# Expert-choice experts of a one-core layer: second half of an expert's inputs made inside its up projection, all down weights split

## The chip, the cores and the metric

One core of a Trainium2 chip runs one launch of the whole layer in fp32. The metric is the device time of that launch in microseconds (us). TensorE is called PE, VectorE DVE, ScalarE ACT, GpSimd POOL, and SP is the engine that issues most DMA loads.

## What is computed

One hybrid layer: a short gated convolution over 1024 tokens of width 2048, followed by 16 experts that each choose 128 tokens. Only the experts matter here.

```python
aff = softmax(h @ w_router)
g, idx = top_k(aff.T, 128)                       # 128 tokens for each of the 16 experts
xe = h[idx]                                      # (16, 128, 2048), h = modulate(rmsnorm(x))
y = (silu(xe @ w1) * (xe @ w3)) @ w2 * g         # w1, w3: 2048x1024, w2: 1024x2048 for each expert
out = rmsnorm(x + g2 * zeros.at[idx].add(y))
```

## The kernel before, in words

The weights of an expert are 48 chunks of 128 x 1024 fp32 numbers (512 KB each): 32 for the up projection, in 16 blocks of two (one of w1, one of w3), and 16 for the down projection, in two halves of 8 blocks of one. The order of all 768 chunks is up(0), up(1), down(0), up(2), down(1), ..., up(15), down(14), down(15), written out by hand; every engine runs its instructions in the order in which the program gives them.

SP loads a chunk into a buffer of a ring of 28 (`c_load`, L1142), 22 chunks ahead of its use from the third expert on, 24 to 26 ahead before. A chunk is then **split** (`c_split`, `split`): ACT rounds it to a high part (`hi`, L76), DVE subtracts that from the raw chunk for a low part (`lo`, L77). `next_chunk` keeps the splits 3 chunks ahead of the matmuls (`SL`). `use_chunk` makes six matmuls of 128 x 512 of a split chunk (L1390: two with the high part, two with the low part, two with the high part and the low part of the inputs). A few chunks are left **unsplit**: their two products go straight from the raw chunk (L1385; the profile shows each fp32 product as two matmul records). Unsplit are 16 chunks of up(0), 4 of up(1), the two of block 1 in every later up projection, and block 7 of each half of every down projection (`NATD = 7`), 32 chunks in all of the down projections.

The inputs of an expert are picked by `select` (DVE compares slot numbers with positions, `oh`, L1318; PE turns that into token numbers, L1321), fetched by `gather` (two indirect DMAs of POOL, L1336, 1024 columns each), scaled by `gathered` (ACT, L1342) and turned by `xe_part`. One `xe_part` makes a quarter, 512 of the 2048 input columns: four PE transposes (L1359), four ACT activations that modulate (`xe`, L1376), one ACT cast (`hi<-xe`, L76) and one DVE subtraction (`lo<-xe`, L77). The first two quarters serve blocks 0 to 7 of the up projection, the last two blocks 8 to 15. Quarters 0 and 2 also take three buffers from the ring of 28.

Such steps hang as hooks behind a block. In down(e), behind blocks 3 and 5, the rows of expert e+2 are scaled; behind blocks 7, 9, 11 and 13 its four quarters are made. In up(e), behind block 8, `select(e+1)` runs, behind block 12 `gather(e+1)`, behind blocks 13 and 14 `hid_part(e-1)`, which turns the middle activations of the expert before (L1409 to L1416). `gate_up` (L1398, L1399) ends an up projection; behind each half of a down projection DVE weights the result (`y`, L1462) and POOL adds it to the stream in DRAM (L1468). In the start, up(0) scales the rows of expert 1 behind its last block, and the four quarters of expert 1 stand between up(0) and up(1). The last rows of the stream are read back (L1561), combined and normalised behind the last expert.

Of the kernel before, what the change touches and what calls it, by code (L numbers as in the profile page):

```python
# [7 lines left out]
F32 = mybir.dt.float32  # L8
# [7 lines left out]
P = 128  # L16
N = 1024
D = 2048
E = 16
F = 1024  # L20
# [3 lines left out]
KF = F // P  # L24
# [10 lines left out]
def hybrid_layer(ctx: ExitStack, tc: tile.TileContext, x, c, w_ada, b_ada, norm_g, w_in, w_conv, w_out,  # L35
                 w_router, w1, w3, w2, final_g, out):
    nc = tc.nc
# [9 lines left out]
    def slot(dtype=F32, name="s", tag="s"):  # L47
        return slots.tile([P, 1024], dtype, name=name, tag=tag, bufs=TAGS[tag])
# [12 lines left out]
    def acc_bank():  # L61
        return psum.tile([P, 512], F32, name="acc", tag="acc", bufs=6)

    def tr_bank():
        return psum.tile([P, 512], F32, name="tr", tag="tr", bufs=2)
# [7 lines left out]
    def split(raw, hi=None, lo=None):  # L73
        hi = part("hi") if hi is None else hi
        lo = part("lo") if lo is None else lo
        nc.scalar.copy(hi, raw)  # L76
        nc.vector.tensor_sub(lo, raw, hi.bitcast(F32))  # L77
        return hi, lo
# [491 lines left out]
    def emit(jp, i):  # L570
        t, b = conv[1].pop(i), conv[2].pop(i)
        nc.vector.tensor_mul(t, b, t)
        nc.gpsimd.dma_start(zd[2 * jp + i], t)
# [93 lines left out]
    for s in range(8):  # L667
        def f(s=s):
            if s:
                make_lo(0, ORDER[s - 1])  # L670
            if s < 7:
                make_sum(0, ORDER[s])
                make_hi(0, ORDER[s])
# [221 lines left out]
    mp = ctx.enter_context(tc.tile_pool(name="moe", bufs=2))  # L895
# [4 lines left out]
    ps = tr_bank()  # L900
# [205 lines left out]
    chunks = []  # L1106
# [6 lines left out]
    def down_chunks(e):  # L1113
        for hf in range(2):
            for k in range(KF):
                chunks.append((w2, e * F * D + k * P * D + hf * 1024, D, k == NATD))


    NAT = (1,)
    NAT1 = (1, 5)  # L1120
    NATD = 7
    NAT0 = (1, 3, 5, 7, 9, 11, 13, 15)
    up_chunks(0)
    for e in range(1, E):
        up_chunks(e)
        down_chunks(e - 1)
    down_chunks(E - 1)

    def is_nat(i):
        return chunks[i][3]  # L1130
# [5 lines left out]
    def c_load(tag="s"):  # L1136
        i = nload[0]
        if i >= len(chunks):
            return
        src, off, stride, _ = chunks[i]  # L1140
        t = slot(name="craw", tag=tag)
        nc.sync.dma_start(t, dram(src, off, [stride, P], [1, 1024]))  # L1142
        craw[i] = t
        nload[0] += 1

    def c_split():
        i = nsplit[0]
        if i >= len(chunks):
            return
        if not is_nat(i):  # L1150
            chl[i] = split(craw.pop(i))
        nsplit[0] += 1
# [176 lines left out]
    def half_rows(name):  # L1329
        return own(name)  # L1330

    def gather(e):
        idx = info[e][1]
        xg[e] = [half_rows("xg") for _ in range(2)]
        for hf in range(2):
            nc.gpsimd.indirect_dma_start(out=xg[e][hf], out_offset=None, in_=x1d[hf][:, :],  # L1336
                                         in_offset=bass.IndirectOffsetOnAxis(ap=idx[:, :1], axis=0))

    def gathered(e, hf, b=None):
        g = xg[e][hf] if b is None else xg[e][hf][:, b * 512:(b + 1) * 512]  # L1340
        if e:
            nc.scalar.activation(g, g, AF.Copy, scale=info[e][0][:, 3:4])  # L1342
        else:
            nc.vector.tensor_scalar(g, g, info[e][0][:, 3:4], None, op0=OP.mult)
# [4 lines left out]
    def xe_part(e, b, quick=False):  # L1349
        if b == 0:  # L1350
            xe[e] = []
        if b % 2 == 0:
            xe[e].append([slot(name="xe"), slot(F32R, "hi"), slot(F32R, "lo")])
        t, hi, lo = xe[e][b // 2]
        g = xg[e][b // 2]
        ps = tr_bank()
        for i in range(4):
            k = (4 * b + i) % 8
            nc.tensor.transpose(ps[:, i * P:(i + 1) * P], g[:, k * P:(k + 1) * P], ident)  # L1359
        if quick:  # L1360
            for i in range(5):
                if i < 4:
                    k = 4 * b + i
                    s = slice((k % 8) * P, (k % 8 + 1) * P)
                    nc.vector.tensor_scalar(t[:, s], ps[:, i * P:(i + 1) * P], G2[:, k:k + 1], S2[:, k:k + 1],
                                            op0=OP.mult, op1=OP.add)
                    nc.scalar.copy(hi[:, s], t[:, s])  # L1367
                if i:
                    k = 4 * b + i - 1
                    s = slice((k % 8) * P, (k % 8 + 1) * P)  # L1370
                    nc.vector.tensor_sub(lo[:, s], t[:, s], hi[:, s].bitcast(F32))
            return
        for i in range(4):
            k = 4 * b + i
            s = slice((k % 8) * P, (k % 8 + 1) * P)
            nc.scalar.activation(t[:, s], ps[:, i * P:(i + 1) * P], AF.Identity, bias=S2[:, k:k + 1],  # L1376
                                 scale=G2[:, k:k + 1])
        s = slice((b % 2) * 512, (b % 2 + 1) * 512)
        split(t[:, s], hi[:, s], lo[:, s])

    def use_chunk(i, banks, sf, sh, sl, first, last):
        if is_nat(i):
            w = craw.pop(i)
            for b in range(2):
                mm(banks[b], sf, w[:, b * 512:(b + 1) * 512], start=first, stop=last)  # L1385
            return
        wh, wl = chl.pop(i)
        for w, a, f, l in ((wh, sh, first, False), (wl, sh, False, False), (wh, sl, False, last)):
            for b in range(2):
                mm(banks[b], a, w[:, b * 512:(b + 1) * 512], start=f, stop=l)  # L1390

    hmid, hT2, hnat = {}, {}, {}

    def gate_up(e, ab, ub):
        hm = slot(name="hm", tag="w")
# [6 lines left out]
    def hid_part(e, b):  # L1402
        if b == 0:
            hT2[e] = (slot(F32R, "hh"), slot(F32R, "hl"))
        hh, hl = hT2[e]
        hm = hmid[e]
        ps = tr_bank()
        for i in range(4):
            nc.tensor.transpose(ps[:, i * P:(i + 1) * P], hm[:, (4 * b + i) * P:(4 * b + i + 1) * P], ident)  # L1409
        n = 384 if NATD // 4 == b else 512  # L1410
        s = slice(b * 512, b * 512 + n)
        nc.scalar.copy(hh[:, s], ps[:, :n])
        nc.vector.tensor_sub(hl[:, s], ps[:, :n], hh[:, s].bitcast(F32))
        if n < 512:
            hnat[e] = mp.tile([P, P], F32, name="hn")
            nc.scalar.copy(hnat[e], ps[:, n:])  # L1416

    step = [0]

    def kcap(i):  # L1420
        return 26 if i < 32 else 24 if i < 64 else K

    def next_chunk():
        i = step[0]
        step[0] += 1
        while nsplit[0] <= min(i + SL, len(chunks) - 1):
            c_split()
        for _ in range(2):
            if nload[0] - i < kcap(i):
                c_load()  # L1430
        return i
# [14 lines left out]
    def seg_down(e, hooks, emit):  # L1446
        hh, hl = hT2[e]
        for hf in range(2):
            yb = [acc_bank() for _ in range(2)]
            for k in range(KF):  # L1450
                s = slice(k * P, (k + 1) * P)
                use_chunk(next_chunk(), yb, hnat[e], hh[:, s], hl[:, s], k == 0, k == KF - 1)
                for f in hooks.get(8 * hf + k, ()):
                    f()
            emit(hf, yb)
        hT2.pop(e)
# [42 lines left out]
    def up_hooks(e):  # L1499
        h = {k: [] for k in range(KD)}  # L1500
        if e < E:
            h[8].append(lambda: select(e))
            h[KG].append(lambda: gather(e))
        h[KH].append(lambda: hid_part(e - 2, 0))
        h[KH + 1].append(lambda: hid_part(e - 2, 1))
        return h

    h = {k: [] for k in range(KD)}
# [5 lines left out]
    h[9].append(place_1)  # L1514
    h[10].append(place_2)
    h[11] += [lambda: select(1), lambda: gather(1)]
    h[15] += [lambda: gathered(1, 0), lambda: gathered(1, 1)]
    seg_up(0, h)
    for b in range(4):
        xe_part(1, b)  # L1520
    h = up_hooks(2)
    g2b = [slot(name="g2b", tag="a") for _ in range(2)]
    for b in range(4):
# [2 lines left out]
    for e in range(E - 2):  # L1526
        h = {k: [] for k in range(16)}
        h[3].append(lambda: gathered(e + 2, 0))
        h[5].append(lambda: gathered(e + 2, 1))
        for b in range(4):  # L1530
            h[7 + 2 * b].append(lambda b=b: xe_part(e + 2, b))
        down_scatter(e, h)
        seg_up(e + 2, up_hooks(e + 3))

# [2 lines left out]
    oht = slot(F32R, "oht")  # L1537
    h = {k: [] for k in range(16)}
    h[3].append(lambda: hid_part(L, 0))
    h[4].append(lambda: hid_part(L, 1))  # L1540

# [90 lines left out]
    h = {k: [] for k in range(16)}  # L1632
# [3 lines left out]
    h[13].append(lambda: combine_0(0))  # L1636
    h[15].append(lambda: combine_0(1))
    seg_down(L, h, last_emit)

    for ch in range(NC_ + 2):  # L1640
# [32 lines left out]
```

## Time and profile before

| | |
|---|---|
| time, median of 3 runs | 2727.5 us (2726.78 to 2733.08) |
| the profiled execution's own time | 2732.52 us |
| its span, first to last instruction | 2730.4 us |
| mean granted TensorE clock | 0.983 |
| busy share of PE, DVE, ACT, POOL | 97%, 76%, 54%, 11% |
| up(0) ends, up(1) starts in it | 1559.67, 1567.36 us |

A row of the chain or of a timeline has the start in us from the span's start, the duration in us, the engine with the line of the kernel, and the count of merged instructions; in brackets the idle time before it and what ended it. A PE record's duration is modelled and overlaps the next; distances between starts are exact.

### The profile page before, as it was taken

How to read it: one execution, taken by the hardware profiler on the slowest of the kernel's cores; microseconds unless marked ns; L12 is line 12 of the kernel's file. 1: busy time of each engine (PE TensorE's matmuls, PEld its weight loads, DVE VectorE, ACT ScalarE, POOL GpSimd, SP SyncE). 2: the span in 40 equal slices, each digit the busy share in tenths (PEclk: the TensorE clock that was granted, in tenths of full speed). 3: DMA queues.
4: the chain of work that ended last, by engine and by line, in shares of the span. 5: the costliest groups of instructions: out<-in, count | busy, mean ns of one | idle time of the engine just before them, and what ended most of it. 6: DMA issues, size and time to landing. Idle time of an engine off the chain costs nothing. (4 is left out here: it accounts for less than half of the span.)

```text
span 2730.4 us, 34249 instructions
## 1 busy us (share of the span) xinstructions
PE 2638.1 (97%) x11641; PEld 2067.4 (76%) x11641; DVE 2078.0 (76%) x2635; ACT 1484.3 (54%) x2142; POOL 291.4 (11%) x319
## 2 busy tenths in 40 slices
PE   6899999989999999999999899999999999999997
PEld 3588778767887887888887577777777777777775
DVE  4688788747877776676567678888888888888887
ACT  6533344423333333333343577777777777777775
POOL 1000111101111010100011000111111101111001
PEclk8899999999999999999998999999999999999999
DMA  9477777686777657897677689999999999999996
GB/s 357 153 240 240 253 271 264 241 318 187 203 203 192 179 121 228 292 301 267 217 266 247 242 324 383 374 373 375 375 372 376 373 372 374 374 373 382 375 347 246
DMA packets 321791, 795.25 MB, mean 291 GB/s; under 512 B 28256, under 2 KB 116224, under 8 KB 321616
## 3 DMA queue, kind: packets, MB, share of 16 engines
q1 hardware_dynamic: 283600, 665.54, 66.1%
q0 software_dynamic: 35728, 127.33, 17.0%
q8 instruction: 91, 1.49, 0.2%
q14 instruction: 84, 0.69, 0.1%
q10 hardware_dynamic: 2288, 0.21, 0.1%
HBM read 699.64 MB, written 93.33 MB: 290 GB/s over the span
## 5 line engine op out<-in xcount | busy, mean ns | idle before, releaser
L77 DVE TENSOR_TENSOR lo<-craw,hi 128x1024 fp32r<-128x1024 f32 x688 | 815.9, 1222 | 90.2 <-ACT hi L76 61.0
L532 PE MATMUL acc<-sh,wp 128*128 128x512 f32 x2872 | 777.6, 396 | 21.4 <-DVE c L617 7.1
L76 ACT CAST hi<-craw 128x1024 fp32r<-128x1024 f32 x688 | 694.9, 1051 | 181.1 <-PE acc L1390 177.0
L532 PEld LDWEIGHTS acc<-sh,wp 128*128 128x128 f32 x2872 | 544.4, 190 | 152.2 <-DVE c L617 11.1
L518 DVE TENSOR_TENSOR wp<-win,wp 128x512 fp32r<-128x512 f32 x336 | 231.5, 689 | 163.0 <-ACT wp L514 160.3
L514 ACT CAST wp<-win 128x512 fp32r<-128x512 f32 x336 | 207.4, 621 | 256.0 <-PE acc L532 122.9
L1390 PE MATMUL acc<-hi 128*128 128x512 f32 x928 | 306.1, 411 | 0.9 <-ACT hi L1367 0.9
L1390 PE MATMUL acc<-lo,hi 128*128 128x512 f32 x928 | 289.5, 393 | 3.4 <-DVE lo L77 1.7
L1390 PE MATMUL acc<-hi,lo 128*128 128x512 f32 x928 | 286.8, 390 | 0.0
L190 DVE SCALAR_TENSOR_TENSOR ada_acc<-wa,silu_c,ada_acc 128x512 f32<-128x512 f32 x338 | 252.9, 749 | 38.7 <-DMA wa<-w_ada 27.7
L612 ACT COPY c<-acc 128x512 f32<-128x512 f32 x156 | 91.6, 587 | 250.1 <-PE acc L532 250.1
L532 PE MATMUL acc<-sl,wp 128*128 128x512 f32 x572 | 224.6, 393 | 0.0
L1390 PEld LDWEIGHTS acc<-lo,hi 128*128 128x128 f32 x928 | 173.1, 188 | 47.1 <-DVE lo L77 11.0
L1390 PEld LDWEIGHTS acc<-hi 128*128 128x128 f32 x928 | 171.2, 189 | 47.8 <-issue 16.7
L925 PE MATMUL acc<-hi 128*128 128x512 f32 x512 | 204.0, 399 | 0.0
L1390 PEld LDWEIGHTS acc<-hi,lo 128*128 128x128 f32 x928 | 174.5, 188 | 37.9
L926 PE MATMUL acc<-lo,hi 128*128 128x512 f32 x512 | 199.6, 390 | 1.4 <-DVE lo L77 1.4
L927 PE MATMUL acc<-hi,lo 128*128 128x512 f32 x512 | 199.7, 390 | 0.0
L77 DVE TENSOR_TENSOR lo<-woraw,hi 128x1024 fp32r<-128x1024 f32 x96 | 116.9, 1220 | 98.6 <-ACT hi L76 50.4
L1390 PE MATMUL acc<-lo,hh 128*128 128x512 f32 x448 | 142.2, 399 | 5.5 <-DVE lo L77 5.5
L1390 PE MATMUL acc<-hi,hh 128*128 128x512 f32 x448 | 144.9, 404 | 0.0
L532 PE MATMUL acc<-sa,wp 128*128 128x512 f32 x576 | 140.8, 393 | 0.0
(246 smaller groups left out, 3206.5 us busy)
## 6 DMA issues: line engine op xcount, KB each, us to landing
craw<-w SPq DMA_DIRECT2D x768, 512.0 KB, 10.2
wa<-w_ada SPq DMA_DIRECT2D x128, 512.0 KB, 6.8
win<-conv_w_in SPq DMA_DIRECT2D x96, 512.0 KB, 6.5
woraw<-conv_w_out SPq DMA_DIRECT2D x96, 512.0 KB, 6.0
wa<-w_ada SPq DMA_DIRECT2D x128, 256.0 KB, 6.0
psums<-c POOLq DMA_DIRECT2D x48, 512.0 KB, 4.4
c<-psums POOLq DMA_DIRECT2D x32, 512.0 KB, 7.7
sh<-sd SPq DMA_DIRECT2D x24, 512.0 KB, 10.8
```

The costliest lines, as they stand in the source:

```text
L76: nc.scalar.copy(hi, raw)
L77: nc.vector.tensor_sub(lo, raw, hi.bitcast(F32))
L190: nc.vector.scalar_tensor_tensor(acc, t[:, a], silu_c[:, k:k + 1], acc, op0=OP.mult, op1=OP.add)
L514: nc.scalar.copy(v3(t[:, :512]), source(u, p))
L518: nc.vector.tensor_sub(v3(lo), source(u, p), v3(hi).bitcast(F32))
L532: mm(bank, w[:, c], a, start=start and q == qs[0] and i == 0, stop=q == qs[-1] and i == 2, skip_group_check=True)
L612: nc.scalar.copy(dst, bk)
L925: mm(bank, zh[:, zs], wh[:, ws], start=k == 0, stop=False)
L926: mm(bank, zh[:, zs], wl[:, ws], start=False, stop=False)
L927: mm(bank, zl[:, zs], wh[:, ws], start=False, stop=k == KD - 1)
L1390: mm(banks[b], a, w[:, b * 512:(b + 1) * 512], start=f, stop=l)
```

## The change

No chunk of a down projection is left unsplit, so block 7 of each half is split like the others. `hid_part` therefore makes the high and low part of all 512 columns and loses the extra copy (L1416). Quarters 0 and 1 of an expert's inputs are made behind blocks 9 and 13 of the down projection, quarters 2 and 3 behind blocks 1 and 4 of the expert's own up projection. For expert 1 the rows are scaled behind block 13 of up(0), quarters 0 and 1 are made behind blocks 14 and 15, and quarters 2 and 3 again behind blocks 1 and 4 of up(1).

```diff
-                chunks.append((w2, e * F * D + k * P * D + hf * 1024, D, k == NATD))
+                chunks.append((w2, e * F * D + k * P * D + hf * 1024, D, False))
...
-        n = 384 if NATD // 4 == b else 512
-        s = slice(b * 512, b * 512 + n)
-        nc.scalar.copy(hh[:, s], ps[:, :n])
-        nc.vector.tensor_sub(hl[:, s], ps[:, :n], hh[:, s].bitcast(F32))
-        if n < 512:
-            hnat[e] = mp.tile([P, P], F32, name="hn")
-            nc.scalar.copy(hnat[e], ps[:, n:])
+        s = slice(b * 512, (b + 1) * 512)
+        nc.scalar.copy(hh[:, s], ps)
+        nc.vector.tensor_sub(hl[:, s], ps, hh[:, s].bitcast(F32))
...
-                use_chunk(next_chunk(), yb, hnat[e], hh[:, s], hl[:, s], k == 0, k == KF - 1)
+                use_chunk(next_chunk(), yb, None, hh[:, s], hl[:, s], k == 0, k == KF - 1)
...
+        h[1].append(lambda: xe_part(e - 1, 2))
+        h[4].append(lambda: xe_part(e - 1, 3))
         h[KH].append(lambda: hid_part(e - 2, 0))
         h[KH + 1].append(lambda: hid_part(e - 2, 1))
...
-    h[15] += [lambda: gathered(1, 0), lambda: gathered(1, 1)]
+    h[13] += [lambda: gathered(1, 0), lambda: gathered(1, 1)]
+    h[14].append(lambda: xe_part(1, 0))
+    h[15].append(lambda: xe_part(1, 1))
     seg_up(0, h)
-    for b in range(4):
-        xe_part(1, b)
...
-        for b in range(4):
-            h[7 + 2 * b].append(lambda b=b: xe_part(e + 2, b))
+        h[9].append(lambda: xe_part(e + 2, 0))
+        h[13].append(lambda: xe_part(e + 2, 1))
```

## Rows read from the trace of the kernel before

**Rows 1.** Windows: down(1) with up(3)'s block 0; then one whole expert period.

```profile
core 0: us, PE busy (x) PEld busy (x) DVE busy (x) ACT busy (x) POOL busy (x), PEclk, DMA share, GB/s
1691.80:1720.31 28.51, 28.00 (x121) 20.87 (x120) 23.67 (x25) 26.73 (x41) 2.34 (x1) 1.00 0.96 344
...
1691.80:1764.36 72.56, 71.88 (x313) 55.60 (x312) 61.21 (x62) 56.10 (x72) 7.12 (x4) 1.00 1.00 376
```

**Rows 2.** Waits from 1650 to 2640: total us, times, longest; ACT, PE's loads, SP.

```profile
ACT hi L76 <- PE acc L1390: 153.3, 242, 2.7
...
PEld acc L1390 <- DVE lo L77: 23.2, 40, 0.9
...
SPq L1142 <- DVE lo L77: 215.4, 165, 8.0
```

**Rows 3.** Chain of waits, in order of time: an unsplit chunk, 24 split ones, transposes.

```profile
2501.25 1.72 PE acc L1385 x4
...
2596.03 32.69 PE acc L1390 x144
2628.72 0.44 PE tr L1409 x4
```

**Rows 4.** Timeline of PE: three chunks of down(1) and up(3) that last longer, and what follows each.

```profile
1695.88 0.61 PE L1390 MATMUL acc<-hi,hh 128*128 128x512 f32 x2
...
1697.49 0.62 PE L1390 MATMUL acc<-hi,hh 128*128 128x512 f32 x2
...
1708.34 0.61 PE L1390 MATMUL acc<-hi,hh 128*128 128x512 f32 x2
...
1710.37 0.60 PE L1359 MATMUL tr<-ident,xg 128*128 128x128 f32 x4
...
1718.52 0.62 PE L1390 MATMUL acc<-hi 128*128 128x512 f32 x2
...
1720.31 3.60 PE L1385 MATMUL acc<-craw,xe 128*128 128x512 f32 x8
```

**Rows 5.** Timelines of PE, ACT and DVE: a first quarter in down(1), later splits in a row.

```profile
1703.31 0.60 PE L1359 MATMUL tr<-ident,xg 128*128 128x128 f32 x4
...
1703.95 1.51 ACT L1376 ACTIVATE xe<-tr,S,G 128x128 f32<-128x128 f32 x4 [1.65 <-PE tr L1359]
1705.49 0.62 ACT L76 CAST hi<-xe 128x512 fp32r<-128x512 f32 x1
1706.01 2.00 ACT L76 CAST hi<-craw 128x1024 fp32r<-128x1024 f32 x2
...
1720.45 5.76 DVE L77 TENSOR_TENSOR lo<-craw,hi 128x1024 fp32r<-128x1024 f32 x5
```

**Rows 6.** Timelines of DVE and PE around `select` in up(3), behind block 8.

```profile
1742.41 1.29 DVE L1318 TENSOR_TENSOR oh<-iot,pos_all 128x512 fp32r<-128x512 f32 x2
...
1742.38 0.61 PE L1390 MATMUL acc<-hi,lo 128*128 128x512 f32 x2
1743.16 1.21 PE L1321 MATMUL tr<-aux,oh 128*128 128x6 f32 x8 [0.17 <-DVE oh L1318]
```

**Rows 7.** Timelines of PE and ACT from up(0)'s last block to up(1)'s block 5.

```profile
1556.24 3.59 PE L1385 MATMUL acc<-craw,xe 128*128 128x512 f32 x8
1559.67 1.04 PE L1359 MATMUL tr<-ident,xg 128*128 128x128 f32 x8
...
1567.36 1.20 PE L1390 MATMUL acc<-hi 128*128 128x512 f32 x2
...
1584.04 3.59 PE L1385 MATMUL acc<-craw,xe 128*128 128x512 f32 x8
...
1557.01 1.15 ACT L1342 ACTIVATE xg<-xg,inf 128x1024 f32<-128x1024 f32 x1 [7.50 <-DMA xg<-x1d,idx]
1559.54 1.15 ACT L1342 ACTIVATE xg<-xg,inf 128x1024 f32<-128x1024 f32 x1 [1.38 <-DMA xg<-x1d,idx]
```

**Rows 8.** Windows with PE's granted clock: two short idle stretches and what follows one.

```profile
1500.10:1502.50 2.40, 0.94 (x5) 0.49 (x3) 1.15 (x4) 0.00 (x0) 0.00 (x0) 1.00 1.01 396
...
1560.20:1563.80 3.60, 0.51 (x5) 0.27 (x3) 1.16 (x2) 3.57 (x7) 0.00 (x0) 1.00 0.01 2
1563.80:1570.60 6.80, 5.12 (x16) 4.05 (x17) 1.51 (x3) 6.70 (x17) 0.00 (x0) 0.50 0.00 0
```

More of the change, by code (lines that the diff above doesn't have):

```diff
@@ L1115, in down_chunks @@
             for k in range(KF):
-                chunks.append((w2, e * F * D + k * P * D + hf * 1024, D, k == NATD))
+                chunks.append((w2, e * F * D + k * P * D + hf * 1024, D, False))
     NAT = (1,)
     NAT1 = (1, 5)
-    NATD = 7
     NAT0 = (1, 3, 5, 7, 9, 11, 13, 15)
@@ L1390, in use_chunk @@
                 mm(banks[b], a, w[:, b * 512:(b + 1) * 512], start=f, stop=l)
-    hmid, hT2, hnat = {}, {}, {}
+    hmid, hT2 = {}, {}
     def gate_up(e, ab, ub):
```

## The prediction

> **What bounds the kernel.** I read the windows first. An expert period, from one down projection to the next, takes 72.56 us, and PE is busy 71.88 of them, at the full granted clock [rows 1]. The weights don't hold it up: in the list of waits from 1650 to 2640, ACT never waits for a weight's DMA; its large wait is for PE to free split buffers (153.3 us), and SP itself waits 215.4 us for ring buffers [rows 2]. So PE sets the pace, and the question is which of PE's time is work and which is waiting. Work: a split chunk takes 32.69 / 24 = 1.36 us, an unsplit one 1.72, four transposes 0.44 [rows 3]. Waiting: PE's weight loads wait 40 times for DVE's low part in these 13.6 periods, so about three times in each [rows 2]. The PE timeline shows the three: one chunk takes 1697.49 - 1695.88 = 1.61 us, one 2.03, one 1.79 [rows 4]; over 1.36 that is 0.25 + 0.67 + 0.43 = 1.35 us. All lie in the down projection or at once behind it, where ACT is busy 26.73 of 28.51 us [rows 1]: the four quarters crowd there. A fourth wait is at `select` in the up projection: PE ends its chunk at 1742.38 + 0.45 = 1742.83 and starts at 1743.16, when DVE's first half of `oh` is done; 0.33 us [rows 6].
>
> **The change, part by part.**
>
> **Unsplit chunks go.** 32 chunks cost PE 1.72 - 1.36 = 0.36 us less each [rows 3]: **-11.5 us**, all on PE's path. The Trainium skill, "FP8 and Floating Point Precision", section TensorE Precision Notes, gives a true fp32 product four passes; against the three of a split chunk that would be a third of 1.36, 0.45 a chunk and -14.5 in all. The row has the duration, so the sum keeps 11.5.
>
> The added work is 64 instructions, 32 casts and 32 subtractions, 1.0 us on ACT and 1.15 on DVE (2.00 / 2 and 5.76 / 5 in a row) [rows 5]. It lies beside PE's work as long as ACT and DVE fit into a down projection. That stretch (18 chunks, now with two quarters) is 18 x 1.36 + 0.88 = 25.4 us of PE. ACT loses two quarters (2.06 each: 1703.95 to 1706.01) and gains two casts: 26.7 - 4.1 + 2.0 = 24.6. DVE gains two subtractions and loses two of a quarter (0.7 each, an estimate from 1.29 / 2 of the same width [rows 6]): 23.7 + 2.3 - 1.4 = 24.6 [rows 1, 5]. It fits, barely. `hid_part` swaps a copy for wider operations, under 0.2 us on ACT and DVE each; hidden by ACT's waits of [rows 2], 16 x 0.2 = 3 us if not.
>
> **Quarters leave the down projection.** With ACT relieved, and `y` (two instructions of DVE behind blocks 7 and 15) no longer in front of a weight split that a quarter has already delayed, I expect the three waits to go: 14 down projections x 1.35 = **-18.9 us**. But each of the four quarters of a period leaves a tie. From the start of its transposes ACT begins 0.64 us later, the quarter's cast 2.18, the next weight's cast 2.70 [rows 5]; that is done at 3.7, its low part at about 5.0. PE has its transposes and three chunks in hand and wants that low part at 0.44 + 3 x 1.36 + 0.45 = 4.97. I take 0.05 us of waiting each: 4 x 14 x 0.05 = **+2.8**, with 0 and 0.15 (+8.4) as ends.
>
> **What is late next: `select`.** This is the step that decides. Quarter 3 now stands behind block 4 of the up projection, `oh` behind block 8, and DVE is in order: eight weights' low parts lie between. Counted from the end of block 4, PE reaches `select` after 0.44 + 8 x 1.36 = 11.3 us. DVE can't begin the first of the eight before ACT has made the quarter and cast the next weight, 3.7 us; then eight at 1.15 make 12.9, and half of `oh` 13.5 [rows 5, 6]. PE waits 2.2 us where it waited 0.33: +1.9 in each of up(2) to up(14). Today DVE has the whole stretch from block 0 to 8 to catch up, at 1.36 - 1.15 = 0.2 us a chunk; after, it starts again at block 4. In up(1), two unsplit chunks in block 5 give PE 0.7 more to do: +1.2. up(15) has no `select`. 13 x 1.9 + 1.2 = **+25.9 us**. Behind PE's wait nothing else is queued that isn't three chunks ahead.
>
> **The start.** Today PE ends up(0) at 1559.67 and starts up(1) at 1567.36, seven microseconds for four quarters [rows 7], part of them and the first matmuls at a granted clock of 0.50, the 1.2 GHz level [rows 8]. After, ACT meets the scaling two blocks earlier, but the rows land no sooner: it is held until 1557.01 and 1559.54 [rows 7], with up(1)'s first two casts now queued behind it. So PE waits at quarter 0 from 1556.24 to about 1558.1, does its last block (3.43) and transposes until 1562.5, and gets quarter 0 and the first chunk at about 1563.7 (scaling until 1560.6, cast 1.0, quarter 2.1). From there I count to block 5's start, all four quarters made: 2 x 1.36 + 2 x 1.72 + 6 x 1.36 + 0.88 = 15.2, and 1.1 for two low parts that come late, 1580.0 against 1584.04: **-4.0**. Ends: -7.7 (the whole gap), and +2 if the rows land later.
>
> **Other queues.** A quarter issues no DMA; what moves is its three ring buffers. Quarter 2 takes them eight blocks or more later, so SP is held no longer than today. POOL's gather stands behind block 12, eight blocks past the last read of the old rows. Both cost nothing, covered by SP's 215.4 us of waiting for buffers [rows 2].
>
> **Sum:** -11.5 - 18.9 + 2.8 + 25.9 - 4.0 = -5.7 us. On the profiled execution (2732.5, of which the span is 2730.4) that is 2726.8; it ran 5.0 above the median, so on 2727.5 I predict **2722**.
>
> **Rivals.**
>
> *No new wait.* DVE is busy only 61.21 of 72.56 us [rows 1]; with two more subtractions 63.5 of some 70. If an average with 6 us to spare is what counts, `select` costs nothing more: 2721.8 - 25.9 = 2696. The Trainium skill, "Perfetto Trace Analysis", section Identifying the Most-Contended Engine, goes by such an occupancy and would have DVE wait for others. Against it: order, not load, puts `oh` behind eight subtractions, and 0.33 us is already lost there [rows 6]. Chance 0.12.
>
> *The ties turn into waits.* The down projection holds 24.6 us of ACT and of DVE in 25.4, and every quarter leaves none to spare. If each of the 56 waits 0.43 us, as the third of [rows 4] does, it is 56 x 0.38 = +21 against my sum: 2743, slower. It decides from 0.15 us each on (0.05 + 5.7 / 56). For it: three of four quarters today leave a wait. Against: the longest of them has `y` in between. Chance 0.09.
>
> *The clock falls.* In the start, PE had almost no work from 1560.2 to 1563.8 and the granted clock then was 0.50 for 6.80 us; after 2.40 us with little work at 1500.1 it stayed at 1.00 [rows 8]. Were it to fall behind each of 14 waits, 14 x 3.4 = +48: 2770. The Trainium skill, "TensorE: Matmul & The Clock Gate", Part 1, lets an idle engine's clock fall and so speaks against a change that adds a wait. The new wait is nearer to the 2.40: chance 0.03.
>
> My forecast: 0.76.
>
> **Numbers.** The forecast's own ends: -5.7 with the start at -7.7, no ties and `select` at 1.5 each (-5) gives 2710; with ties of 0.15 and a start of 0 it is 2731. The rivals hold 0.24; to leave out no more than 0.2 the range reaches down to the edge of the first: 2698 to 2732. A measurement of this kernel tells 0.3% from nothing, 8.2 us. Faster than 2719.3: the first rival and 0.37 of the forecast, 0.40. Slower than 2735.7: the other two rivals, less what of the second stays below it, 0.11. The rest, 0.49, is within.
>
> **What would show it.** Right: no record at L1385 with `hn`; `PEld acc L1390 <- DVE lo` far below 40 times; `PE tr L1321 <- DVE oh` at some 2 us each, 13 times, where it was 0.33; DVE without a gap from block 4 to `oh`; up(1) starting about 4 us after up(0) ends. Wrong: a period near 70 us without that wait (first rival), waits for the low part behind blocks 9 and 13 of the down and 1 and 4 of the up projection (second), or a granted clock below 1.00 behind block 8 (third).

## The result: slower, by a wait that was foreseen and a clock that was given next to no chance

The changed kernel takes **2743.2 us** in the median of 6 runs, the kernel before 2732.5 in 6 runs beside it: ratio **1.0053, 95% interval [1.0041, 1.0065]**, which on 2732.5 is 14.5 us slower (the two medians are 10.7 apart). I had predicted 2722 in a range of 2698 to 2732, so the time lies outside the range and on the other side of no change. The profiled execution of after took 2750.52 us with a span of 2747.8; its mean granted clock is 0.979, before 0.983. It is the second longest of the six, which go from 2741.57 to 2754.63 us at clocks of 0.981 to 0.977, so the trace shows some us more of the loss than the median has.

The loss lies in the expert periods. One row of the trace brackets them: the activations of the middle (`hm`, ACT), two in each of up(1) to up(15). The view gives the instructions of one tile: count, shortest, median and longest duration in ns, then first and last start. First before, then after:

```profile
L1398 ACT ACTIVATE hm<-acc x30: 592/596/602, 1619.8 to 2636.2; 128x512 f32<-128x512 f32 x30
```

```profile
L1397 ACT ACTIVATE hm<-acc x30: 590/597/601, 1620.7 to 2654.4; 128x512 f32<-128x512 f32 x30
```

Before, this stretch lasts 2636.2 - 1619.8 = 1016.4 us, after 2654.4 - 1620.7 = 1033.7: +17.3, all but 0.1 of the 17.4 by which the spans differ. I call it **the stretch** and use it for every kernel below.

The waits of after from 1650 to 2640 (engine and line, what it waited for: us in total, times, longest):

```profile
PEld tr L1320 <- DVE oh L1317: 30.2, 13, 2.3
...
PE tr L1320 <- DVE oh L1317: 24.7, 13, 1.9
...
PEld acc L1389 <- DVE lo L77: 16.5, 54, 0.3
...
SPq L1141 <- DVE lo L77: 535.3, 431, 5.6
```

Three things answer to [rows 2]. PE's loads wait for low parts 54 times instead of 40, but never over 0.3 us where it was 0.9: the three long waits of a down projection are gone, and four small ones have come. At `select` PE waits 13 times, 24.7 us in all. And SP waits 535.3 us for ring buffers that DVE frees, more than the 215.4 of before, and for the weights' own DMAs 66.3 us in all, so the weights are still well ahead.

At `select` this is what the timelines of DVE and PE show (start us, duration us, engine, line, operation, count; idle time before it in brackets):

```profile
1811.70 9.18 DVE L77 TENSOR_TENSOR lo<-craw,hi 128x1024 fp32r<-128x1024 f32 x8 [0.25 <-ACT hi L76]
1820.79 1.28 DVE L1317 TENSOR_TENSOR oh<-iot,pos_all 128x512 fp32r<-128x512 f32 x2
...
1746.14 0.61 PE L1389 MATMUL acc<-hi,lo 128*128 128x512 f32 x2
1748.66 1.21 PE L1320 MATMUL tr<-aux,oh 128*128 128x6 f32 x8 [1.91 <-DVE oh L1317]
1749.73 0.71 PE L1389 MATMUL acc<-hi 128*128 128x512 f32 x2
...
1819.04 0.61 PE L1389 MATMUL acc<-hi,lo 128*128 128x512 f32 x2
1821.53 1.21 PE L1320 MATMUL tr<-aux,oh 128*128 128x6 f32 x8 [1.87 <-DVE oh L1317]
...
1823.86 1.06 PE L1389 MATMUL acc<-hi,lo 128*128 128x512 f32 x2
1824.71 1.06 PE L1389 MATMUL acc<-hi 128*128 128x512 f32 x2
...
1893.50 0.61 PE L1389 MATMUL acc<-hi,lo 128*128 128x512 f32 x2
1896.02 1.21 PE L1320 MATMUL tr<-aux,oh 128*128 128x6 f32 x8 [1.91 <-DVE oh L1317]
```

Eight low parts in a row stand ahead of `oh` on DVE, as the prediction counted. PE's chunk ends at 1819.04 + 0.45 = 1819.49 and `select` starts at 1821.53: 2.04 us, at the other two 2.07, where [rows 6] had 0.33. But look at what follows: behind the second `select` a pair of matmuls lasts 1.06 us that lasted 0.61 before it. PE has gone to half speed. Windows of 8 us behind the `select` of up(3) to up(5) (stretch; busy us and instructions of PE, PEld, DVE, ACT, POOL; granted clock; DMA share; GB/s):

```profile
1750.00:1758.00 8.00, 8.00 (x36) 6.57 (x36) 7.45 (x10) 5.18 (x5) 3.43 (x2) 1.00 1.03 410
1823.00:1831.00 8.00, 8.00 (x30) 6.46 (x29) 6.12 (x6) 4.21 (x4) 2.46 (x2) 0.79 1.02 408
1897.00:1905.00 8.00, 8.00 (x31) 6.44 (x31) 5.94 (x8) 3.69 (x4) 2.48 (x2) 0.79 1.03 410
```

Of the 14 windows behind a `select`, four have 1.00, nine 0.79 and one (up(2), from 1674) 0.63: part of each of these ten was granted at 0.50, the 1.2 GHz level. A shorter window behind the second `select` above shows it:

```profile
1824.00:1826.00 2.00, 2.00 (x7) 1.54 (x6) 1.47 (x2) 1.04 (x1) 1.70 (x2) 0.50 1.03 410
```

What that costs can be read from the starts above. From the first `select`, with no fall behind it, to the second are 1821.53 - 1748.66 = 72.87 us; from the second, with one, to the third 1896.02 - 1821.53 = 74.49. A fall costs **1.6 us**. The windows say much the same: 8 x (1 - 0.79) = 1.7, and 8 x (1 - 0.63) = 3.0 for the longer one.

### The profile page after: what moved, and what is told of

Same layout as the page of the kernel before. It is cut to its first block, busy times and chain, and to the rows that moved or that the text cites. A ratio compares the mean times of both kernels' runs of the same rounds, so it can differ in the third digit from the quotient of the medians.

```text
span 2747.8 us, 34476 instructions
## 1 busy us (share of the span) xinstructions
PE 2639.4 (96%) x11705; PEld 2087.4 (76%) x11705; DVE 2106.7 (77%) x2667; ACT 1502.0 (55%) x2158; POOL 291.8 (11%) x319
## 4 chain that ended last, share of the span: by engine, by line
PE 54%; DVE 3%; DMA 3%; ACT 2%; issue 1%; POOL 0%; POOLq 0%; DVEq 0%; ACTq 0%
PE acc L1389 33%; PE acc L925 4%; PE acc L927 4%; PE acc L926 4%; PE acc L1384 3%; DMA craw<-w 2%; PE acc L532 2%; DVE lo L77 2%; PE tr L1358 1%; PE acc L979 1%; PE tr L1320 1%; ACT hi L76 1%; ACT xe L1375 1%; PE tr L968 1%; PE tr L1408 1%
## 5 line engine op out<-in xcount | busy, mean ns | idle before, releaser
L77 DVE TENSOR_TENSOR lo<-craw,hi 128x1024 fp32r<-128x1024 f32 x720 | 841.7, 1221 | 74.6 <-ACT hi L76 56.2
L76 ACT CAST hi<-craw 128x1024 fp32r<-128x1024 f32 x720 | 711.3, 1051 | 109.7 <-PE acc L1389 104.6
L1389 PE MATMUL acc<-lo,hi 128*128 128x512 f32 x928 | 299.4, 405 | 1.1 <-DVE lo L77 1.1
L1389 PE MATMUL acc<-hi,lo 128*128 128x512 f32 x928 | 293.4, 398 | 0.0
L926 PE MATMUL acc<-lo,hi 128*128 128x512 f32 x512 | 199.6, 390 | 1.4 <-DVE lo L77 1.4
L927 PE MATMUL acc<-hi,lo 128*128 128x512 f32 x512 | 199.7, 390 | 0.0
L1389 PE MATMUL acc<-hi,hh 128*128 128x512 f32 x512 | 161.2, 396 | 0.0
L1389 PE MATMUL acc<-lo,hh 128*128 128x512 f32 x512 | 159.7, 393 | 0.0
L1389 PE MATMUL acc<-hi,hl 128*128 128x512 f32 x512 | 158.0, 390 | 0.0
## 6 DMA issues: line engine op xcount, KB each, us to landing
sh<-sd SPq DMA_DIRECT2D x24, 512.0 KB, 10.8
```

The source lines that it names most:

```text
L926: mm(bank, zh[:, zs], wl[:, ws], start=False, stop=False)
L927: mm(bank, zl[:, zs], wh[:, ws], start=False, stop=k == KD - 1)
```

## The experiments

My theory after the result: the wait at `select` is there because `oh` stands behind eight low parts on DVE, the clock's falls follow from it, and without both the change would be a gain. The rival: what the change adds, more splits and four quarters among them, is the loss. The table has the result of each run, and the stretch from the trace of each.

| kernel | median us | ratio to before, 95% interval | stretch us |
|---|---|---|---|
| after | 2743.2 | 1.0053 [1.0041, 1.0065] | 1033.7 |
| a_moves_only | 2768.48 | 1.013 [1.0113, 1.0147] | 1623.4 to 2679.0: 1055.6 |
| b_split_only | 2734.39 | 1.001 [0.9998, 1.0021] | 1618.3 to 2639.5: 1021.2 |
| c_fill | 2730.43 | 0.9995 [0.9986, 1.0005] | 1620.2 to 2637.7: 1017.5 |
| d_oh_early | 2701.62 | 0.9895 [0.9879, 0.9912] | 1614.0 to 2601.9: 987.9 |
| e_start_undone | 2743.47 | 1.0041 [1.0028, 1.0054] | 1620.5 to 2650.8: 1030.3 |
| f_split_ahead | 2691.74 | 0.9855 [0.984, 0.987] | 1617.4 to 2594.8: 977.4 |
| g_quarter_late | 2697.91 | 0.9873 [0.9858, 0.9888] | 1616.1 to 2603.7: 987.6 |
| h_unsplit_kept | 2712.46 | 0.9929 [0.9915, 0.9942] | 1619.8 to 2620.4: 1000.6 |
| i_both | 2685.96 | 0.9834 [0.9821, 0.9847] | 1613.0 to 2590.4: 977.4 |
| j_all_split | 2679.4 | 0.9807 [0.9794, 0.9819] | 1615.6 to 2584.3: 968.7 |
| j_repeat, the same kernel | 2679.25 | 0.981 [0.9794, 0.9826] | 1617.1 to 2585.8: 968.7 |

### c_fill: the wait stays, PE is kept busy in it

Four products of a constant with the identity, whose result nothing reads, stand ahead of each of these `select`s, so that PE works while it would wait. `hold(4)` makes them.

```diff
-            h[8].append(lambda: select(e))
+            h[8] += [lambda: hold(4), lambda: select(e)]
```

> The changed kernel with four matmuls without a use (256 columns of fp32 each, about 0.43 us) ahead of `select` in each up projection that has one. Theory: the loss is made of PE's wait of 2.07 us at `select`, of the granted clock that falls to 0.50 behind it in ten of fourteen places, and of about 0.18 us at each quarter. The four matmuls lie inside the wait, so `select` starts when it did, but PE is not idle and the clock stays at 1.00: 10 to 11 stretches of 3.41 us at half rate go, 16 to 18 us, from 2743 to about 2726. Rival (the 32 added splits are the loss, the clock only shows it): 2743, within 4.

Measured: 0.9995 [0.9986, 1.0005], 2730.43 us. The PE timeline around the `select` of up(4), and the window behind it:

```profile
1815.85 1.89 PE L1257 MATMUL acc<-wr,ident 128*128 128x256 f32 x8
1817.92 1.21 PE L1320 MATMUL tr<-aux,oh 128*128 128x6 f32 x8 [0.18 <-DVE oh L1317]
1818.99 0.70 PE L1389 MATMUL acc<-hi 128*128 128x512 f32 x2
```

```profile
1819.00:1827.00 8.00, 8.00 (x37) 6.63 (x37) 7.41 (x9) 5.01 (x5) 3.44 (x2) 1.00 1.03 407
```

`select` starts no earlier within its period, for it still waits for `oh`; but all 14 windows behind it now have 1.00, and the stretch is 1033.7 - 1017.5 = 16.2 us shorter. So with the wait kept and the falls gone the kernel is back where before was, and the falls of the clock are what made it slower. The wait itself is unchanged: the time between PE's last useful product and `select` is 2.08 us here (1815.39 + 0.45 to 1817.92) and 2.04 to 2.07 in after.

### d_oh_early: the wait taken away

DVE compares for `oh` behind block 1 of the up projection, ahead of quarter 2; PE's part and everything behind it stays at block 8.

```diff
...
+    def select_early(e):
+        oh_t[e] = slot(F32R, "oh", "w")
+        for b in range(2):
+            one_hot(e, pos_all[:, :, e], b)
...
+            h[1].append(lambda: select_early(e))
             h[8].append(lambda: select(e))
             h[KG].append(lambda: gather(e))
         h[1].append(lambda: xe_part(e - 1, 2))
```

`one_hot` is the comparison that stood in `select`.

> The changed kernel with DVE's two `oh` instructions of `select` moved from behind block 8 to behind block 1 of the up projection, ahead of quarter 2, where DVE sits idle for 2.64 us; PE's matmuls of `select` stay behind block 8. Theory: PE no longer waits at `select` (2.07 us, 14 times, 28 us in all) and the clock doesn't fall there (17 us): 2743 - 45 = 2698; the four ties of 0.18 us stay. Rival (the added splits are the loss): the time stays above 2730, the wait goes to the low parts.

Measured: **0.9895 [0.9879, 0.9912]**, 2701.62 us, faster than both kernels. The timelines of DVE and PE in up(4):

```profile
1781.36 3.48 DVE L77 TENSOR_TENSOR lo<-craw,hi 128x1024 fp32r<-128x1024 f32 x3
1784.77 1.28 DVE L1309 TENSOR_TENSOR oh<-iot,pos_all 128x512 fp32r<-128x512 f32 x2
1787.49 0.69 DVE L77 TENSOR_TENSOR lo<-xe,hi 128x512 fp32r<-128x512 f32 x1 [1.44 <-ACT hi L76]
...
1804.62 0.62 PE L1400 MATMUL acc<-hi,lo 128*128 128x512 f32 x2
1805.07 0.95 PE L1331 MATMUL tr<-aux,oh 128*128 128x6 f32 x8
1805.88 0.72 PE L1400 MATMUL acc<-hi 128*128 128x512 f32 x2
```

The comparisons lie where DVE had to wait for the quarter anyway, and 1.44 us of that idle time are still left. PE starts `select` 0.45 us after the last chunk's last pair, at once, and its eight products take 1805.88 - 1805.07 = 0.81 us instead of 1749.73 - 1748.66 = 1.07, the second half of `oh` being there too. No clock falls at a `select`: from 1660 to 2640 the granted clock is 1.00. One instruction pair, moved by seven blocks, is worth 1033.7 - 987.9 = 45.8 us of the stretch: 16.2 by the clock (c_fill); for the rest, 29.6, 13 waits of 2.07 and 13 times 0.26 would make 30.3. The early comparison alone, on the kernel before, was not run; its waits at `select` there (3.8 us in all, 13 times) leave it little to gain.

### a_moves_only and b_split_only: one half of the change each

`a_moves_only` makes the quarters at the new places and keeps the unsplit weights; `b_split_only` splits all and leaves the quarters behind blocks 7, 9, 11 and 13 and the start as they were. The hunks of a_moves_only, on the kernel before:

```diff
+        h[1].append(lambda: xe_part(e - 1, 2))
+        h[4].append(lambda: xe_part(e - 1, 3))
...
-    h[15] += [lambda: gathered(1, 0), lambda: gathered(1, 1)]
+    h[13] += [lambda: gathered(1, 0), lambda: gathered(1, 1)]
+    h[14].append(lambda: xe_part(1, 0))
+    h[15].append(lambda: xe_part(1, 1))
     seg_up(0, h)
-    for b in range(4):
-        xe_part(1, b)
...
-        for b in range(4):
-            h[7 + 2 * b].append(lambda b=b: xe_part(e + 2, b))
+        h[9].append(lambda: xe_part(e + 2, 0))
+        h[13].append(lambda: xe_part(e + 2, 1))
```

Those of b_split_only, with the matching ones in `hid_part`:

```diff
-                chunks.append((w2, e * F * D + k * P * D + hf * 1024, D, k == NATD))
+                chunks.append((w2, e * F * D + k * P * D + hf * 1024, D, False))
```

> The kernel before with the moved quarters and the start of the change, but block 7 of each down half left unsplit. Theory: quarter 3 at block 4 still puts `oh` late, so PE's wait of 2.07 us at `select` and the falling clock stay; PE has 32 x 0.36 = 11.5 us more of matmuls, DVE two subtractions less in each down projection, which may take away half of the ties (5 us): 2748 to 2755, slower than before by 16 to 22 us. Rival (the added splits are the loss): 2720 to 2732.

> The kernel before with every down chunk split and nothing moved. Theory: no wait at `select` beyond the 0.45 us of before and no falling clock; but ACT has 26.7 + 2.0 = 28.7 us in a down projection of 18 x 1.36 + 4 x 0.44 = 26.2 us of PE, so the stretch takes as long as ACT, about as today (28.5): the 11.5 us that PE saves are waited away, 2725 to 2738, no change. Rival (the added splits are the loss): 2745 or more.

Measured: the moves alone 1.013 [1.0113, 1.0147], slower than the whole change and above what I expected. Behind its first, second and eighth `select` the windows of a_moves_only show:

```profile
1599.00:1607.00 8.00, 8.00 (x35) 6.44 (x35) 3.61 (x6) 4.91 (x6) 2.89 (x2) 0.79 1.03 412
1676.00:1684.00 8.00, 8.00 (x24) 6.48 (x25) 4.50 (x7) 1.25 (x2) 2.45 (x2) 0.60 1.03 410
...
2130.00:2138.00 8.00, 8.00 (x24) 6.40 (x24) 5.06 (x7) 2.97 (x3) 2.79 (x2) 0.60 1.03 409
```

Here the clock fell behind all 14, and the window has 0.60 in three of them, although the waits at `select` are the same as in after (24.6 us, 13 times, to 24.7). Its stretch is 21.9 us longer than after's. Of that, 28 unsplit chunks at 0.36 us [rows 3] to 0.45 (h_unsplit_kept below) are 10 to 13. The rest is of the size of the clock: 13 falls in the stretch, three of them longer, where after has nine, one of them longer, are some 9 us more at 1.6 a fall and 3 a longer one.

The split alone is the kernel before within its interval (1.001). The waits of b_split_only say why it brings nothing:

```profile
PE acc L1389 <- DVE lo L77: 15.1, 39, 0.5
...
PEld acc L1389 <- DVE lo L77: 31.8, 39, 1.0
```

Before, its loads waited 23.2 us, 40 times [rows 2]. With the quarters still crowded into the down projection, PE waits for low parts what it saves in passes. So neither half does anything good by itself; the rival, that the added splits are the loss, falls with 1.001.

### h_unsplit_kept: what the unsplit chunks are worth once the wait is gone

`d_oh_early` with the unsplit weights of the down projections back (the matching ones in `hid_part` are not shown).

```diff
-                chunks.append((w2, e * F * D + k * P * D + hf * 1024, D, False))
+                chunks.append((w2, e * F * D + k * P * D + hf * 1024, D, k == NATD))
```

> d_oh_early, with the down projections' unsplit weights kept as before (the moves alone, with the comparisons early). Theory (an unsplit block costs 0.36 us more on TensorE, 32 of them 11.5 us, and the quarters at their new places leave VectorE time for the splits): 8 to 14 us above d_oh_early, ratio to before 0.9925 to 0.995. Rival (b_split_only, where all split gave nothing, holds here too: the splits take on VectorE and ScalarE what TensorE saves): within 4 us of d_oh_early, 0.988 to 0.991.

Measured: 0.9929 [0.9915, 0.9942]. Its stretch is 1000.6 - 987.9 = 12.7 us longer for 28 chunks, 0.45 each. The ratios differ by 0.0034, some 9 us for all 32, the medians by 10.8. So the prediction's 11.5 us lie in the middle of what was measured; the stretch gives more than its 0.36 a chunk, and what adds the rest there isn't shown.

### e_start_undone: the start

The changed kernel with expert 1's four quarters between up(0) and up(1), as before, which also takes quarters 2 and 3 out of up(1).

```diff
-        h[1].append(lambda: xe_part(e - 1, 2))
-        h[4].append(lambda: xe_part(e - 1, 3))
+        if e > 2:
+            h[1].append(lambda: xe_part(e - 1, 2))
+            h[4].append(lambda: xe_part(e - 1, 3))
...
-    h[13] += [lambda: gathered(1, 0), lambda: gathered(1, 1)]
-    h[14].append(lambda: xe_part(1, 0))
-    h[15].append(lambda: xe_part(1, 1))
+    h[15] += [lambda: gathered(1, 0), lambda: gathered(1, 1)]
     seg_up(0, h)
+    for b in range(4):
+        xe_part(1, b)
```

> The changed kernel, with expert 1's four quarters made behind expert 0's up projection as before. The trace of after puts block 5 of expert 1's up projection only 0.9 us earlier than before. Theory (the move at the start gains next to nothing, since the second block there waits for the banks of expert 0's activation, which stands behind the quarters): 0 to +2 us on the changed kernel's time, ratio to the kernel before 1.005 to 1.007. Rival (the prediction's term): +4 us or more, ratio 1.007 to 1.009.

Measured: 2743.47 us, 1.0041 [1.0028, 1.0054], the same as after within the intervals and a little under the expected 1.005 to 1.007. That total doesn't price the start by itself, because without quarter 3 in up(1) the wait at up(1)'s `select` goes too. The timelines of PE show both. First the `select` in up(0) of before, which no edit moves; then the same and the `select` of up(1) in after; then both in e_start_undone, with block 5 between them:

```profile
1546.18 1.21 PE L1321 MATMUL tr<-aux,oh 128*128 128x6 f32 x8 [0.35 <-DVE oh L1318]
```

```profile
1546.24 1.21 PE L1320 MATMUL tr<-aux,oh 128*128 128x6 f32 x8 [0.35 <-DVE oh L1317]
...
1596.28 1.21 PE L1320 MATMUL tr<-aux,oh 128*128 128x6 f32 x8 [1.38 <-DVE oh L1317]
```

```profile
1548.34 1.21 PE L1320 MATMUL tr<-aux,oh 128*128 128x6 f32 x8 [0.35 <-DVE oh L1317]
...
1585.64 3.59 PE L1384 MATMUL acc<-craw,xe 128*128 128x512 f32 x8
...
1597.70 1.21 PE L1320 MATMUL tr<-aux,oh 128*128 128x6 f32 x8 [0.29 <-DVE oh L1317]
```

From that `select` to block 5 of up(1) are 1584.04 - 1546.18 = 37.86 us before, 1583.12 - 1546.24 = 36.88 in after and 1585.64 - 1548.34 = 37.30 here: the new start gains 1.0 us on the old one, 0.4 by this run. Then up(1)'s `select` takes it back: after waits there (1.38 in the bracket against 0.29), and the window behind it has 0.79, in this run 1.00. So this run, which is 2.1 us later at the first of the two, is only level at up(1)'s activation (1620.5, in after 1620.7) because it gains 2.3 us between them.

The trace of after shows where the 4 us went that the prediction had here. Its timelines of PE and ACT:

```profile
1562.43 0.74 PE L1389 MATMUL acc<-hi 128*128 128x512 f32 x2 [0.50 <-ACT hi L76]
...
1563.48 0.62 PE L1389 MATMUL acc<-hi,lo 128*128 128x512 f32 x2
1567.34 1.28 PE L1389 MATMUL acc<-hi 128*128 128x512 f32 x2 [3.24 <-ACT hm L1397]
...
1583.12 1.45 PE L1384 MATMUL acc<-craw,xe 128*128 128x512 f32 x3
...
1563.24 1.49 ACT L1375 ACTIVATE xe<-tr,S,G 128x128 f32<-128x128 f32 x4
1564.76 0.62 ACT L76 CAST hi<-xe 128x512 fp32r<-128x512 f32 x1
1565.40 1.28 ACT L1397 ACT_TABLE_LOAD   x1
1566.69 1.09 ACT L1397 ACTIVATE hm<-acc 128x512 f32<-128x512 f32 x2
```

PE starts up(1) at 1562.43, five microseconds earlier than in [rows 7], but its second chunk (the first of w3) needs banks that up(0)'s activation `hm` has yet to read. `hm` stands on ACT behind quarter 1, and a table load of 1.28 us stands ahead of it. PE waits 3.24 us, comes back at half speed (1.28 us for a pair), and reaches block 5 at 1583.12 against 1584.04. The gap was moved, not closed.

### f_split_ahead, g_quarter_late, i_both: the ties, and the second quarter of expert 1

`f_split_ahead` is d_oh_early with the next weight's split put between a quarter's transposes and its activations. `g_quarter_late` is d_oh_early with expert 1's quarter 1 behind block 0 of up(1). `i_both` has both.

```diff
+        if e > 1:
+            c_split()
         for i in range(4):
             k = 4 * b + i
...
-    h[15].append(lambda: xe_part(1, 1))
     seg_up(0, h)
     h = up_hooks(2)
+    h[0].append(lambda: xe_part(1, 1))
```

> d_oh_early, with the split of one more weight put ahead of the quarter's four activations on ScalarE, so that the next blocks' weights don't stand behind the quarter. Theory (each of the four quarters of a period costs 0.16 to 0.20 us per following block since TensorE waits for a low part that VectorE makes behind the quarter): the row of TensorE waiting on the low part's subtraction (16.3 us, 53 times) falls to under 5 us and the time by 6 to 12 us on d_oh_early: ratio to before 0.985 to 0.9875. Rival (the lost time is not the order of the queues but ScalarE's and VectorE's load around a quarter, so it only moves to the next blocks): same as d_oh_early within 3 us, 0.9885 to 0.9905.

> d_oh_early, with expert 1's second quarter made behind block 0 of its own up projection in place of the last block of expert 0's, so that expert 0's activation has one quarter less ahead of it on ScalarE. Theory (the second block of expert 1's up projection waits for the banks that this activation frees): that wait shrinks from about 3 us to under 2, and the time by 1 to 3 us on d_oh_early, ratio 0.988 to 0.9895. Rival (the table load and the activation itself hold the banks): within 1 us of d_oh_early, ratio about 0.989 to 0.99.

> d_oh_early with both edits, the split put ahead of a quarter's activations (f_split_ahead, ratio 0.9855) and expert 1's second quarter behind block 0 of its own up projection (g_quarter_late, 0.9873). Theory (the two act at different places, so their gains add: d_oh_early's spans 2695.9 less 7.1 is 2688.8 with the first; the second moved block 5 of expert 1's up projection by no gain in its trace, and the ratio's intervals overlap with d_oh_early's): 2686 to 2691 us, ratio 0.983 to 0.986. Rival (the second quarter in block 0, with a split ahead of it, delays the next weights): 1 to 3 us slower than f_split_ahead, 0.986 to 0.987.

Measured: 0.9855 [0.984, 0.987], 0.9873 [0.9858, 0.9888] and 0.9834 [0.9821, 0.9847]. PE's loads in the waits of d_oh_early, then all that is left of them in f_split_ahead:

```profile
PEld acc L1395 <- issue: 18.7, 78, 0.2
PEld acc L1400 <- DVE lo L77: 16.3, 53, 0.3
PEld tr L1369 <- issue: 6.9, 26, 0.3
```

```profile
PEld acc L1397 <- issue: 18.7, 78, 0.2
PEld tr L1369 <- issue: 6.9, 26, 0.3
```

The row of the low parts is gone, and the stretch is 987.9 - 977.4 = 10.5 us shorter: the 56 quarters had cost 10.5 / 56 = **0.19 us** each. The ties are a matter of order, not of load, since the same work is done in both kernels.

The late quarter lies ahead of the stretch, and the intervals of g_quarter_late and d_oh_early overlap, so I don't count its gain as shown by itself. i_both is in its expected 2686 to 2691 and its stretch is f_split_ahead's to the tenth.

### j_all_split, run twice: no unsplit weights in the later up projections either

`i_both` with `NAT = ()`, 28 more chunks split.

```diff
-    NAT = (1,)
+    NAT = ()
```

> i_both, and no unsplit weights in the up projections of experts 2 to 15 either: 28 blocks more with three passes. Theory (TensorE is never idle in the middle of f_split_ahead's trace, so 0.36 us less of TensorE a block is time saved): 28 times 0.36 is 10 us less than i_both, ratio near 0.98. Rival (VectorE, 251 us busy of 280 in f_split_ahead's middle, gets 28 more subtractions of 1.22 us, and the DMA engines, whose share there is 1.03, leave no room for a shorter period): the period stays at 69.8 us and TensorE waits on low parts or ScalarE on weights instead; ratio within 0.002 of i_both.

> j_all_split once more, unchanged: one of its six times was 5158 us, the other five between 2675 and 2684. If that one was a disturbance from outside the kernel, all times here lie between 2673 and 2686 and the ratio is again 0.980 to 0.982; if the kernel's order of work has a second course, another time far above shows up.

Measured: 0.9807 [0.9794, 0.9819] and, again, 0.981 [0.9794, 0.9826] (2673.54 to 2684.4 us), with the same stretch. One of the six times of the first was 5158 us; it is not in the ratio, none of the five repeats was like it, and what it was is open. The stretch is 977.4 - 968.7 = 8.7 us shorter of 10 expected. The waits of j_all_split from 1650 to 2640, of SP and of PE's loads; then SP's own row of before, which [rows 2] does not have:

```profile
SPq L1141 <- DMA craw<-w: 418.6, 435, 3.1
SPq L1141 <- DVE lo L77: 231.8, 272, 3.5
...
PEld acc L1402 <- DVE lo L77: 3.1, 13, 0.2
```

```profile
SPq L1142 <- DMA craw<-w: 445.2, 426, 3.4
```

Thirteen small waits for a low part have come. What limits this kernel next is not shown: SP waits much for the weights' own DMAs (418.6 us, against 66.3 in after), but before had 445.2 of the same, and ACT waits for a weight 4.0 us in all. This is the fastest kernel of the study, 52 us below before.

## Why the prediction was wrong

Its sum was -5.7 us; the stretch and the start came to +17.4 in the profiled spans, +14.5 by the ratio. Term by term:

- **Unsplit chunks, -11.5: right in the main.** h_unsplit_kept gives 9 by the ratios, 10.8 by the medians and 0.45 a chunk by the stretch, which for 32 would be 14.5. The four passes of the Trainium skill, "FP8 and Floating Point Precision", section TensorE Precision Notes, gave the prediction its other estimate, 0.45 a chunk and 14.5. The stretch agrees with that, the totals are nearer to the sum's 11.5, and the chunk by itself lasts 1.72 us [rows 3], less than the 1.81 of four thirds of 1.36.
- **The three low-part waits, -18.9: right in kind.** None over 0.3 us is left. The parts of d_oh_early's gain on the stretch are 28 x 0.45 = 12.7, these 18.9, 13 x 0.45 at `select` and 13 x 0.26 in its products, less 10.5 of ties. They come to 30.3; measured are 1016.4 - 987.9 = 28.5, so some 17 of the 18.9 came.
- **The ties, +2.8: mis-sized.** "I take 0.05 us of waiting each", ends 0 and 0.15; f_split_ahead gives 0.19, +10.5, outside both ends. The working had PE want the low part at 4.97 and DVE deliver at about 5.0, two sums of five durations each; a margin of 0.03 us between such sums has no sign, and the upper end should have been a good part of a subtraction of 1.15. The rival on the ties was half right: 0.19 lies past the 0.15 from which it decides, and far below its 0.43.
- **`select`, 2.2 us of wait: right.** 2.04 to 2.07 in the rows, eight low parts and half of `oh` as counted. For up(2) to up(14) the view of waits has 24.7 us of it against 3.8 before, +20.9 where the prediction had 13 x 1.9 = 24.7: the row taken for before was one of its shorter waits (0.17 in its bracket [rows 6], 3.8 / 13 = 0.29 in the mean, which with what the brackets leave out is some 0.45). In up(1) it had 1.2, and the bracket rose from 0.29 to 1.38. The occupancy rival (2696) is refuted: PE waits on a DVE that the page has busy for 77% of the span. By the Trainium skill, "Perfetto Trace Analysis", section Identifying the Most-Contended Engine, the engine to work on first is the one with the highest occupancy. DVE, at 77% against PE's 96%, is not that one, and the gain of d_oh_early came from the order on it.
- **The start, -4.0: wrong.** -1.0 in the trace. "From there I count to block 5's start" left out that up(1)'s w3 products need banks that `hm` frees, and that `hm` now stood behind two quarters.
- **The clock, put at nothing in the sum: the step that failed.** "The new wait is nearer to the 2.40: chance 0.03." The comparison was of unlike stretches: in the 2.40 us of [rows 8] PE still worked 0.94 us, so that it did nothing for some 1.5, while in the 2.07 us of the new wait it does nothing throughout. One stretch that stayed at 1.00 could not carry such a chance either; waits of one length went both ways here. And the price was too high, which made the rival look absurd: 3.4 us a fall, from the one long stretch at the start, when a fall here costs 1.6. In its place the runs showed nine falls in the stretch, one of them longer, that made 16.2 us (c_fill). With the right price, the rival of 14 falls would have stood at 2722 + 14 x 1.6 = 2744. That this lies beside the 2743.2 that came is luck: ten fell, and the errors of the other terms (ties +7.7, start +3.0, `select` some -4) are not in that rival.

So the mechanism that decided was in the text, as a rival with next to no chance. Without the clock the change is worth nothing (c_fill, 0.9995), since the larger ties and the lost start eat the 5.7 us of the sum. The Trainium skill, "TensorE: Matmul & The Clock Gate", Part 1, lets an idle engine's clock fall and was the warning to heed; ten of the 14 windows agree with it, four don't.

## What to carry to other kernels

When work is moved to where it "fits", look at what stands behind it on each in-order engine up to the next hand-over to PE: here one pair of comparisons behind eight subtractions cost more than all the rest gained, and moving that pair ahead turned 1.0053 into 0.9895. Price a new wait of PE with the clock's fall behind it, at about the 1.6 us that the rows show here, and don't put the chance of a fall near nothing: here ten of 14 such waits had one. Two edits that each do nothing or harm (1.001 and 1.013) can be worth over a per cent together once a third thing is out of the way, so look for that third thing before either is dropped.

## What the runs showed of the hardware

- Behind waits of some 2.05 us at `select` the granted clock fell to 0.50 in nine of 13 places in after, in all 13 in a_moves_only and in eight of 13 in e_start_undone; behind the shorter wait of up(1) (1.38 in after's bracket) it fell in after and in a_moves_only. Waits of the same length (1746.59 to 1748.66, and 1893.95 to 1896.02 in after) went both ways; what tells them apart is open.
- It never fell behind `select` when PE did products without a use for most of the wait (c_fill, 14 windows at 1.00), and the falls gone were worth 16.2 us while the wait itself stayed.
- A DMA share of 1.03 was no limit yet in f_split_ahead (392 GB/s from 1850 to 2130): with the same weights to load, j_all_split made its stretch of 977.4 us 8.7 shorter. Whether that kernel's own share is a limit isn't shown.
